# Moments by ScalarE for the first four token tiles, and a norm without GpSimd's long step for the last four, in the ConvFFN of a two-layer encoder

## The chip, the cores and the metric

One core of one Trainium2 chip. The metric is device microseconds of one execution of the program, as a median over runs; the profile is one more execution with the hardware profiler on.

## The reference

The model is a two-layer post-norm encoder over 1024 tokens of width 1024, in float32. Each layer is an attention mixer and then a ConvFFN, each with a residual and a LayerNorm behind it. The change touches the LayerNorm behind the ConvFFN, once in each layer:

```python
def _layer_norm(x, g, b):
    mu = jnp.mean(xf, axis=-1, keepdims=True)
    var = jnp.mean(jnp.square(xf - mu), axis=-1, keepdims=True)
    y = (xf - mu) * lax.rsqrt(var + LN_EPS)
    return y * g + b
...
x = _layer_norm(DN_ALPHA * x + h, ln_attn_g[layer], ln_attn_b[layer])
f = _conv_ffn(x, ffn_w_in[layer], ffn_conv_w[layer], ffn_conv_b[layer], ffn_w_out[layer])
x = _layer_norm(DN_ALPHA * x + f, ln_ffn_g[layer], ln_ffn_b[layer])
```

## The kernel before

The 1024 tokens are eight tiles of 128 rows, `Y[0]` to `Y[7]`, each 128x1024. The down projection of the ConvFFN is made as seven products of a Strassen-like scheme. Each product runs over 11 steps of the contraction, and a step makes 12 matmuls: four token tiles, three matmuls each (high by high, high by low, low by high). The matmuls of a product gather in four PSUM banks, `As` (name `dna`) or `Cs` (name `dnc`). In this text the steps of the last product are called p4(0) to p4(10), after the function that prepares them; the product ahead of it is the one into the second `Cs`.

A step is prepared so: `pair` loads two 128x512 blocks into one tile `pr` by two DMAs from SP's queue (L646); for p4 VectorE then subtracts an earlier block from the second (L713); ScalarE rounds the tile to its high part (L654); VectorE subtracts for the low part (L655). The two parts lie in a tile `opj`, of which there are seven, so preparation runs up to seven steps ahead of TensorE.

The tile `pr` comes from `room`, which goes round a ring of eight buffers with three tags:

```python
def room():
    tag = ("raw", "raw", "whi", "wlo", "whi", "wlo", "whi", "wlo")[ring["pr"] % 8]
    ring["pr"] += 1
    return wpool.tile([P, 2, 512], F32, name="pr", tag=tag, bufs=2 if tag == "raw" else 3)
```

When the last product begins, `room` has been called 64 times, so p4(0) has a buffer of tag raw. The same three tags serve other code: in layer 0 the weights `b_v_weights(0)` for the next layer, which the program asks for behind p4(3), take two buffers of each tag, and hold theirs in whi and wlo until a product long after.

The order of the instructions on each engine and queue is made ahead of time by a planner that plays the program through with planned durations and, whenever an engine is free, places the ready instruction that stands first in the program. A tile has no buffer until its first writer is placed, and the buffers of one tag are given out in the order in which the program asks for them: a tile's first writer is not placed ahead of the first writer of a tile of the same tag asked for earlier. Once placed, an engine keeps its order. `urgent()` moves an instruction some 400 places forward in that order.

At the end of the last `Cs` product `to_y` (L677) adds the four banks to `Y[0]` to `Y[3]`, and `layer_norm` is called for them: two `bn_stats` of 512 columns (L211), `bn_aggr` (L213), two 128x1 steps on GpSimd (L215, L216), two `scalar_tensor_tensor` of 1024 columns on VectorE (L229, L231), and a store (L235). In the program these stand ahead of p4(0). The last product then runs steps 0 to 4 over all four token tiles, and steps 5 to 10 tile by tile. As each bank is finished, `to_y` (L675) and `layer_norm` follow for `Y[4]` to `Y[7]`. For t < 3 in layer 1 (`Y[4]`, `Y[5]`, `Y[6]`) `spread` is true: ScalarE scales and shifts (L225), VectorE multiplies by the gain (L226), GpSimd adds the bias row over 1024 columns (L227). For the others VectorE does L229 and two halves of L231, each stored by itself (L233). In layer 0 `tail` also turns each finished tile by eight transposes (L245, name `tps`) for the next layer.

Of the kernel before, what the change touches and what calls it, by code (L numbers as in the profile page):

```python
# [10 lines left out]
F32 = mybir.dt.float32  # L11
F32R = mybir.dt.float32r
AF = mybir.ActivationFunctionType
ALU = mybir.AluOpType
# [6 lines left out]
P = 128  # L21
S = 1024
D = 1024
# [7 lines left out]
EPS = 1e-5  # L31
# [63 lines left out]
def trunk_kernel(ctx, tc, A):  # L95
    nc = tc.nc
# [18 lines left out]
    sm = ctx.enter_context(tc.tile_pool(name="sm", bufs=6))  # L115
# [29 lines left out]
    mhalf = const.tile([P, 1], F32, name="mhalf")  # L145
# [59 lines left out]
    def moments(y, halves=None):  # L205

        st = sm.tile([P, 2, 6], F32, name="st", tag="st", bufs=3)
        for h in (1, 0) if halves else (0, 1):
            if halves:
                halves(h)  # L210
            nc.vector.bn_stats(st[:, h, :], y[:, h * 512:(h + 1) * 512])  # L211
        mv = sm.tile([P, 2], F32, name="mv", tag="mv", bufs=3)
        nc.vector.bn_aggr(mv, st.rearrange("p a b -> p (a b)"))  # L213
        rs = sm.tile([P, 1], F32, name="rs", tag="rs", bufs=3)
        nc.gpsimd.tensor_scalar(rs, mv[:, 1:2], 1.0, EPS, ALU.mult, ALU.add)  # L215
        nc.gpsimd.tensor_tensor(rs, rs, mhalf, ALU.pow)  # L216
        return mv[:, 0:1], rs

    def layer_norm(y, g_bc, b_bc, out=None, spread=False, halves=None):

        mean, rs = moments(y, halves)
        if spread:
            nm = sm.tile([P, 1], F32, name="nm", tag="nm", bufs=3)
            nc.gpsimd.tensor_scalar(nm, mean, rs, -1.0, ALU.mult, ALU.mult)
            nc.scalar.activation(y, y, AF.Identity, bias=nm, scale=rs)  # L225
            nc.vector.tensor_tensor(y, y, g_bc, ALU.mult)  # L226
            nc.gpsimd.tensor_tensor(y, y, b_bc, ALU.add)  # L227
        else:
            nc.vector.scalar_tensor_tensor(y, y, mean, g_bc, ALU.subtract, ALU.mult)  # L229
            for c in (slice(0, 512), slice(512, D)) if halves else (slice(0, D),):  # L230
                nc.vector.scalar_tensor_tensor(y[:, c], y[:, c], rs, b_bc[:, c], ALU.mult, ALU.add)  # L231
                if halves and out is not None:
                    nc.sync.dma_start(out=out[:, c], in_=y[:, c])  # L233
        if out is not None and (spread or not halves):
            nc.sync.dma_start(out=out, in_=y)  # L235
# [92 lines left out]
    def ffn(layer, op, old, four, xp, tmp, then, out, tail):  # L328
# [222 lines left out]
        room = old.tile([P, 8192], F32R, name="late", tag="xs1")  # L551
# [70 lines left out]
        Y = [fp.tile([P, D], F32, name=f"y{t}") for t in range(NT)]  # L622
        g_bc = fp.tile([P, D], F32, name="g_bc")
        b_bc = fp.tile([P, D], F32, name="b_bc")
# [13 lines left out]
# [4 lines that stand above are left out]
# [20 lines left out]
        def times(ps, o, t, first, last):  # L662
            a, b = [[x[:, 0], x[:, 1]] for x in o] if isinstance(o, list) else [
                [o[:, n, c:c + 512] for c in (0, 512)] for n in range(2)]
            a = [x[:, t * P:(t + 1) * P] for x in a]
            mm3(ps, [(a[0], a[1], b[0], b[1])], first=first, last=last, joined=True)
# [5 lines left out]
        def to_y(t, c, ps, first):  # L672
            with urgent():
                if first:
                    nc.vector.scalar_tensor_tensor(Y[t][:, c], Y[t][:, c], ALPHA, ps, ALU.mult, ALU.add)  # L675
                else:
                    nc.vector.tensor_tensor(Y[t][:, c], Y[t][:, c], ps, ALU.add)  # L677
# [70 lines left out]
            new_x(xp2)  # L748
        for t in range(4):
            to_y(t, lo_, Cs[t], False)  # L750
            layer_norm(Y[t], g_bc, b_bc, out(t))
        for m in range(NM - 6):
            turn(As, p4(m), m)
            if m:
# [2 lines left out]
        for t in range(4):  # L757
            for m, o in enumerate(os):
                times(As[t], o, t, False, m == 5)

            def add(h, t=t):
                if not h:
                    to_y(t + 4, lo_, As[t], True)

            layer_norm(Y[t + 4], g_bc, b_bc, out(t + 4), t < 3 and layer == 1, add)
            tail(t + 4, Y[t + 4], fp)

    def score_tile(W, T, i, q, ka, kb, mask, out, fold):
# [590 lines left out]
    def tail_a(t, y, f):  # L1359
# [6 lines left out]
        if t == 7:  # L1366
            plain(b_v(0, wv0, lambda: 0.0, f, range(0, 4)))
            for p in pend:
                x_from(*p, "SS")

    ffn(0, op, xp, (top, ("hl1", "hl0", "g", "b")), xp2, tmp, then_a, lambda t: x2_d[t], tail_a)
    open_f.pop().close()
    st_xb = open_f.pop()
# [16 lines left out]
    def then_b():  # L1390
# [8 lines left out]
        return x, f  # L1399

    ffn(1, op, xp, (keep, ("rt", "hl", "cosT", "sinT")), xp2, tmp, then_b, lambda t: A["out"][t * P:(t + 1) * P, :],
        lambda t, y, f: None)
    open_f.pop().close()
# [69 lines left out]
```

## Time and profile before

| | |
|---|---|
| median of 3 runs | 2545.67 us (2541.77 to 2546.02) |
| the profiled execution's own time | 2547.09 us |
| its span, first to last instruction | 2545.3 us |
| mean granted TensorE clock | 0.985 |
| busy: TensorE, VectorE, ScalarE, GpSimd | 96%, 74%, 46%, 23% |

A row of a timeline gives the start in us from the span's start, the duration, engine, line, operation and operands, and in brackets the idle time of that engine just before and what ended it. "x4" means that so many like instructions are merged in the row. PE is TensorE, PEld its weight load, DVE VectorE, ACT ScalarE, POOL GpSimd, SP the queue that issues the DMAs.

### The profile page before, as it was taken

The numbers are of one execution on the slowest core, as the hardware profiler recorded it, in microseconds if no ns is written. First come the engines' busy times: TensorE is split into PE (matmuls) and PEld (weight loads), VectorE is DVE, ScalarE is ACT, GpSimd is POOL, SyncE is SP. The second block draws the span as 40 slices with busy tenths as digits, with TensorE's granted clock in tenths as the row PEclk, the third lists the DMA queues.
The fourth block names the chain that finished last, engine by engine and source line by source line (L and its number), as shares of the span: only waits on it lengthen the run. The fifth ranks groups of instructions, "written<-read, shape, count | busy, mean of one in ns | idle before, by whom it ended". The sixth has DMA issues, their size and how long they took to land.

```text
span 2545.3 us, 36019 instructions
## 1 busy us (share of the span) xinstructions
PE 2452.3 (96%) x12784; PEld 2094.7 (82%) x12784; DVE 1888.5 (74%) x3446; ACT 1164.3 (46%) x2077; POOL 588.6 (23%) x670
## 2 busy tenths in 40 slices
PE   8999999899999999999999999998999999999997
PEld 7989898777778888788788898987777888887885
DVE  5656565768887877787858686878688888787877
ACT  3545454533544544443325454544334554544432
POOL 3333332621200000000123536355312000100003
PEclk9999999999999999999999999999999999999998
DMA  7564655634522222755465546454545222228552
GB/s 243 182 215 132 201 157 179 207 113 168 196 105 99 83 79 99 262 181 195 139 205 170 161 144 193 144 181 135 175 158 185 89 96 91 83 87 302 170 194 100
DMA packets 195172, 400.76 MB, mean 157 GB/s; under 512 B 18976, under 2 KB 73248, under 8 KB 193968
## 3 DMA queue, kind: packets, MB, share of 16 engines
q1 hardware_dynamic: 194992, 398.46, 46.8%
q8 instruction: 101, 1.65, 0.3%
q14 instruction: 79, 0.65, 0.1%
HBM read 285.07 MB, written 113.31 MB: 157 GB/s over the span
## 4 chain that ended last, share of the span: by engine, by line
PE 79%; DMA 9%; DVE 6%; POOL 2%; issue 2%; ACT 1%; SPq 1%; POOLq 0%; DVEq 0%; ACTq 0%
PE ua L192 15%; PE pj L192 10%; PE dna L192 8%; PE uc L192 8%; PE vp L192 7%; PE dnc L192 7%; PE op L192 6%; PE ub L192 4%; PE tp L813 3%; DMA t<-in_w_dram 3%; PE sc L783 2%; PE sc L784 2%; PE pv L1211 2%; DMA t1d<-t 1%; PE pv L1007 1%
## 5 line engine op out<-in xcount | busy, mean ns | idle before, releaser
L192 PE MATMUL pj<-x,whi 128*128 128x512 f32 x992 | 322.2, 397 | 0.2 <-DVE rt L1149 0.2
L192 PE MATMUL dna<-opj 128*128 128x512 f32 x1008 | 235.7, 395 | 10.2 <-DVE opj L659 5.7
L192 PEld LDWEIGHTS dna<-opj 128*128 128x128 f32 x1008 | 191.7, 191 | 52.5 <-DVE opj L659 6.6
L192 PEld LDWEIGHTS pj<-x,whi 128*128 128x128 f32 x992 | 184.3, 189 | 34.9 <-issue 0.2
L818 DVE TENSOR_TENSOR tl<-tp,th 128x512 fp32r<-128x512 f32 (+1 forms) x240 | 149.9, 633 | 72.0 <-ACT th L817 67.0
L529 POOL TENSOR_TENSOR he<-he,tg 128x512 f32<-128x512 f32 x22 | 49.2, 2234 | 659.0 <-DVE tg L527 629.0
L192 PE MATMUL vp<-whi,x 128*128 128x256 f32 (+1 forms) x960 | 194.7, 289 | 3.1 <-DVE vt L1107 2.0
L192 PE MATMUL pj<-x,wlo 128*128 128x512 f32 x496 | 197.4, 398 | 0.0
L817 ACT CAST th<-tp 128x512 fp32r<-128x512 f32 (+1 forms) x240 | 127.8, 542 | 129.8 <-PE tp L813 87.3
L192 PE MATMUL dnc<-opj 128*128 128x512 f32 x792 | 180.5, 389 | 0.0
L192 PEld LDWEIGHTS dnc<-opj 128*128 128x128 f32 x792 | 148.7, 188 | 30.8
L192 PE MATMUL op<-wo,oh 128*128 128x512 f32 x512 | 165.7, 404 | 8.3 <-DVE yw L302 3.2
L654 ACT CAST opj<-pr 128x1024 fp32r<-128x1024 f32 x88 | 92.7, 1054 | 152.6 <-PE dna L192 64.2
L813 PE MATMUL tp<-ident_r,pt 128*128 128x128 f32 x864 | 152.8, 278 | 8.7 <-DVE tl L818 6.5
L446 ACT CAST late<-sr 128x512 fp32r<-128x512 f32 x132 | 81.2, 618 | 172.4 <-DVE sr L452 142.0
L192 PEld LDWEIGHTS vp<-whi,x 128*128 128x128 f32 x960 | 154.1, 190 | 6.7 <-DVE vt L1107 2.2
L1001 POOL TENSOR_SCALAR pt<-pt,rr 128x128 f32<-128x128 f32 (+7 forms) x128 | 96.2, 758 | 220.7 <-DVE rr L1000 190.7
L215 POOL TENSOR_SCALAR rs<-mv 128x1 f32<-128x1 f32 x32 | 18.4, 575 | 541.8 <-DVE mv L213 540.9
L783 PE MATMUL sc<-ka,q 128*128 128x512 f32 (+3 forms) x384 | 133.4, 372 | 8.9 <-DVE pt L1185 5.0
L1189 ACT ACTIVATE pt<-pt,mn 128x256 f32<-128x256 f32 (+7 forms) x128 | 98.9, 773 | 86.6 <-DVE mn L794 63.5
L998 ACT ACTIVATE pt<-pt,mn 128x128 f32<-128x128 f32 (+7 forms) x128 | 99.1, 775 | 85.5 <-DVE mn L794 67.1
L192 PE MATMUL vp<-wlo,x 128*128 128x256 f32 (+1 forms) x480 | 138.2, 288 | 0.0
(255 smaller groups left out, 6560.5 us busy)
## 6 DMA issues: line engine op xcount, KB each, us to landing
raw<-in_w_dram SPq DMA_DIRECT2D x88, 512.0 KB, 4.4
pr<-in_w_dram SPq DMA_DIRECT2D x132, 256.0 KB, 3.4
pr<-hd SPq DMA_DIRECT2D x96, 256.0 KB, 3.0
t<-in_w_dram SPq DMA_DIRECT2D x22, 512.0 KB, 3.6
hd<-tg SPq DMA_DIRECT2D x22, 512.0 KB, 3.0
raw<-in_aqk_dram SPq DMA_DIRECT2D x16, 512.0 KB, 4.9
vd<-vt SPq DMA_DIRECT2D x32, 256.0 KB, 2.8
qd<-hl SPq DMA_DIRECT2D x32, 256.0 KB, 3.5
```

The source lines that it names most:

```text
L192: nc.tensor.matmul(ps, a, b, start=first and i == 0, stop=last and i == n - 1, skip_group_check=joined)
L446: nc.scalar.copy(w[:, 0], src)
L654: nc.scalar.copy(o[:, :, 0:512], rs[0])
L783: nc.tensor.matmul(ps[:, :n], q, ka[:, c0:c0 + n], start=True, stop=False)
L784: nc.tensor.matmul(ps[:, :n], q, kb[:, c0:c0 + n], start=False, stop=not dg)
L813: nc.tensor.transpose(tp[:, n * P:(n + 1) * P], pts[q][:, k * P:(k + 1) * P], ident)
L817: nc.scalar.copy(th[:, :n], tp[:, :n])
L818: nc.vector.tensor_tensor(tl[:, :n], tp[:, :n], f32(th[:, :n]), ALU.subtract)
L998: nc.scalar.activation(pt, pt, AF.Exp, bias=mn, scale=-1.0, accum_out=rs)
L1001: nc.gpsimd.tensor_scalar(pt, pt, rr, 1.0, ALU.mult, ALU.mult)
L1189: nc.scalar.activation(pt, pt, AF.Exp, bias=mn, scale=-1.0, accum_out=rs)
L1211: nc.tensor.matmul(o, vv[:, k, v, :], t[:, c], start=(k == 0 and m == 0), stop=(g == j and b == 1 and m == 2))
```

## The change

The first four tiles of each ConvFFN get a norm of their own: ScalarE runs over the tile twice with an accumulated sum (once for the mean, once squared for the variance), GpSimd makes three 128x1 steps, and VectorE's two passes remain. The output of the squaring pass is not needed; it goes to a tile from `room`. For the last four tiles `spread` is now false in both layers.

```diff
+    def layer_norm_act(y, g_bc, b_bc, out, junk):
+        s = sm.tile([P, 4], F32, name="as", tag="as", bufs=3)
+        nc.scalar.activation(y, y, AF.Identity, accum_out=s[:, 0:1])
+        nc.gpsimd.tensor_scalar(s[:, 1:2], s[:, 0:1], -1.0 / D, 0.0, ALU.mult, ALU.add)
+        nc.scalar.activation(junk, y, AF.Square, bias=s[:, 1:2], accum_out=s[:, 2:3])
+        nc.gpsimd.tensor_scalar(s[:, 3:4], s[:, 2:3], 1.0 / D, EPS, ALU.mult, ALU.add)
+        nc.gpsimd.tensor_tensor(s[:, 3:4], s[:, 3:4], mhalf, ALU.pow)
+        nc.vector.scalar_tensor_tensor(y, y, s[:, 1:2], g_bc, ALU.add, ALU.mult)
+        nc.vector.scalar_tensor_tensor(y, y, s[:, 3:4], b_bc, ALU.mult, ALU.add)
+        nc.sync.dma_start(out=out, in_=y)
...
         for t in range(4):
             to_y(t, lo_, Cs[t], False)
-            layer_norm(Y[t], g_bc, b_bc, out(t))
+            layer_norm_act(Y[t], g_bc, b_bc, out(t), room().rearrange("p a n -> p (a n)"))
...
-            layer_norm(Y[t + 4], g_bc, b_bc, out(t + 4), t < 3 and layer == 1, add)
+            layer_norm(Y[t + 4], g_bc, b_bc, out(t + 4), False, add)
```

## Rows read from the trace of the kernel before

**Rows 1.** The page: busy time of each engine, share, instructions.

```profile
PE 2452.3 (96%) x12784; PEld 2094.7 (82%) x12784; DVE 1888.5 (74%) x3446; ACT 1164.3 (46%) x2077; POOL 588.6 (23%) x670
```

**Rows 2.** Chain that ended last, layer 1's end: start us, us, what.

```profile
2466.63 29.92 PE dnc L192 x132
2496.55 29.93 PE dna L192 x132
...
2532.54 1.04 POOL rs L215
...
2537.41 2.82 DVE y L231
```

**Rows 3.** Windows by stage: us, busy us (count) by engine, clock, DMA.

```profile
1239.85:1276.00 36.15, 33.57 (x159) 27.38 (x158) 35.98 (x49) 10.17 (x13) 7.35 (x8) 1.00 0.43 147
...
2496.50:2526.50 30.00, 29.97 (x133) 24.48 (x131) 28.72 (x41) 5.48 (x6) 7.78 (x13) 1.00 0.18 71
2526.50:2545.30 18.80, 0.00 (x0) 0.00 (x0) 11.61 (x9) 3.41 (x3) 12.72 (x10) 0.60 0.28 112
```

**Rows 4.** Timeline of VectorE in layer 1's last stage.

```profile
2521.52 1.28 DVE L675 SCALAR_TENSOR_TENSOR y<-y,dna 128x512 f32<-128x512 f32 x2 [0.82 <-PE dna L192]
...
2530.17 3.36 DVE L229 SCALAR_TENSOR_TENSOR y<-y,mv,g_bc 128x1024 f32<-128x1024 f32 x1
...
2537.41 3.48 DVE L231 SCALAR_TENSOR_TENSOR y<-y,rs,b_bc 128x512 f32<-128x512 f32 x2 [2.74 <-POOL rs L216]
```

**Rows 5.** Timeline of TensorE in layer 0's last product.

```profile
1259.99 1.09 PE L245 MATMUL tps<-ident_r,y 128*128 128x128 f32 x8 [0.94 <-DVE y L231]
1261.67 1.19 PE L192 MATMUL dna<-opj 128*128 128x512 f32 x4 [0.59 <-ACT opj L654]
...
1264.79 5.06 PE L192 MATMUL dna<-opj 128*128 128x512 f32 x21 [1.06 <-DVE opj L655]
```

**Rows 6.** Timeline of SP's queue: layer 1's last load of p4.

```profile
2490.70 0.43 SPq L646 DMA_DIRECT2D pr<-in_w_dram  x1
```

**Rows 7.** Groups by line and form, VectorE, 2490 to 2546: busy us, mean ns.

```profile
L655 DVE TENSOR_TENSOR opj<-pr,opj 128x1024 fp32r<-128x1024 f32 x9 | 10.9, 1208 | 0.0
L211 DVE BATCH_NORM_STATS2 st<-y 128x6 f32<-128x512 f32 x15 | 9.9, 673 | 0.0
...
L231 DVE SCALAR_TENSOR_TENSOR y<-y,rs,b_bc 128x1024 f32<-128x1024 f32 x4 | 5.0, 1269 | 0.0
...
L213 DVE BATCH_NORM_AGGREGATE mv<-st 128x2 f32<-128x12 f32 x8 | 1.6, 194 | 0.0
L713 DVE TENSOR_TENSOR pr<-pr,t 128x512 f32<-128x512 f32 x2 | 1.4, 692 | 1.8 <-DMA pr<-in_w_dram 1.6
```

**Rows 8.** Groups by line, ScalarE, whole span (of L654, 2490 to 2546).

```profile
L998 ACT ACTIVATION_READ_ACCUMULATOR pt<-pt,mn 128x1 f32 x128 | 24.1, 188 | 0.0
L225 ACT ACTIVATE y<-y,nm,rs 128x1024 f32<-128x1024 f32 x5 | 6.1, 1239 | 24.3 <-POOL nm L224 24.3
L515 ACT ACT_TABLE_LOAD x2 | 2.6, 1283 | 6.2 <-DVE tg L512 6.2
...
L654 ACT CAST opj<-pr 128x1024 fp32r<-128x1024 f32 x7 | 7.4, 1055 | 11.7 <-PE dna L192 6.7 <-PE dnc L192 3.3 <-DVE pr L713 1.7
```

**Rows 9.** The page, DMA issues: KB each, median us to landing.

```profile
pr<-in_w_dram SPq DMA_DIRECT2D x132, 256.0 KB, 3.4
```

**Rows 10.** Timeline of GpSimd: its 128x1 step, alone and beside VectorE.

```profile
2502.96 0.19 POOL L215 TENSOR_SCALAR rs<-mv 128x1 f32<-128x1 f32 x1 [182.12 <-DVE mv L213]
...
2507.21 1.11 POOL L215 TENSOR_SCALAR rs<-mv 128x1 f32<-128x1 f32 x1 [0.98 <-DVE mv L213]
```

**Rows 11.** Windows where layer 1's down projection begins.

```profile
2316.00:2320.00 4.00, 1.19 (x4) 0.67 (x4) 3.86 (x5) 3.92 (x8) 0.75 (x1) 1.00 1.05 395
2320.00:2324.00 4.00, 2.55 (x7) 2.03 (x8) 4.00 (x6) 1.53 (x4) 0.84 (x1) 0.77 1.06 389
2324.00:2328.00 4.00, 4.00 (x16) 3.17 (x15) 4.00 (x8) 3.52 (x8) 0.00 (x0) 0.81 1.04 417
```

## The prediction

> **What bounds the kernel now.** I read the page first: TensorE is busy for 96% of the span and no other engine for more than 74% [rows 1]. So an edit on VectorE, ScalarE or GpSimd counts only where TensorE waits for them, and behind its last matmul. I then looked for those places in the two stretches that the diff touches.
>
> In layer 1 there is no wait ahead of the end. The last two products take 29.92 and 29.93 us for 132 matmuls each, which is 0.227 us a matmul with no gap [rows 2]. Then TensorE is done, at 2526.5, and the span goes on for 18.8 us [rows 2, 3]. That tail is VectorE and GpSimd: two banks are only taken up at 2521.5; one L229 takes 3.36 us beside GpSimd's long step, where a pass of 1024 columns alone takes 1.27; and the last L231 waits 2.74 us for a 128x1 step which stood in GpSimd's queue behind such long steps, then takes 3.48 us for its two halves [rows 2, 4, 7].
>
> In layer 0 VectorE is busy for 35.98 of the 36.15 us of the last product, and TensorE stands idle three times, 0.94, 0.59 and 1.06 us, together 2.6 [rows 3, 5].
>
> A third thing is to be seen in SP's queue: the last of p4's loads is issued at 2490.7, 6 us before the product ahead of p4 ends at 2496.55 [rows 2, 6]. The eleven steps of the last product are all fetched early; that is why it starts without a gap.
>
> **The change, part by part.** *VectorE, first four tiles.* Eight L211 and four L213 a layer go: 8 x 0.67 + 4 x 0.19 = 6.1 us [rows 7]. In layer 1 that is off the path, since TensorE did not wait; in layer 0 it can at most give back the 2.6 us.
>
> *ScalarE, first four tiles.* Each gets two passes. The nearest row is L225's pass of 1024 columns, 1.24 us, and an accumulated sum adds an instruction of 0.19 [rows 8]: 1.43 us a pass, eight passes, 11.4 us a layer. ScalarE has the time on average; the question is what is queued behind them. Square may also need a table load, of which the trace does not show whether it is due behind Silu: between 0 and 1.28 us a layer [rows 8]. I take 0, because Identity of L225 ran behind Silu without one, and keep both ends. The Trainium skill (ScalarE: Activation LUTs, section "What ACT_TABLE_LOAD costs") puts a switch of sets at about 2.66 us, the drain included. By that page the sum would be up to 5.3 us more; the row shows only the 1.28 of the load itself.
>
> *The buffer for the squares.* This is the part that decides. `room` is called four times more, ahead of p4(0). By the ring, the four squaring outputs take raw, raw, whi, wlo, and p4(0) to p4(10) now get whi, wlo, whi, wlo, raw, raw, whi, wlo, whi, wlo, whi. Buffers of a tag are given out in program order, and a tile's first writer is not placed ahead of that of an earlier tile of its tag. So the load of p4(0) is placed behind the third tile's Square, that of p4(1) behind the fourth's, and p4(4) and p4(5) behind the first two. These loads were out 6 us before the end of the product ahead; now they are placed after it.
>
> How late: call E the end of the product ahead. Its first bank is finished nine matmuls before E (9 x 0.227 = 2.0 us), and `to_y` takes 0.64 [rows 2, 4], so ScalarE starts at E - 1.4. A Square needs the mean of its own tile through GpSimd, 0.19 to 1.11 us for the step [rows 10], so the planner puts another tile's pass in between: Identity 0, 1, Square 0, 1, Identity 2, 3, Square 2, 3. The third Square starts after six passes, at E - 1.4 + 8.6 = E + 7.2. Then p4(0) needs two issues (0.43 each at most) and 3.4 us to land [rows 6, 9], L713 0.69, L654 1.06: TensorE's first matmul at E + 13.2. From below: SP need not wait for the third Square itself, only for what stands ahead in its queue, the loads of p4(4) and p4(5), which need the first two Squares done (E + 4.3); then ScalarE's own queue sets it, eight passes to E + 10.0 and the rounding, 11 us. From above: with the roundings of p4(4) and p4(5) ahead (2.1 us) 15.3, and the low part of p4(0) comes 1.2 us after [rows 7, 8]. I take a gap of 12.5 us in each layer, range 11 to 16.
>
> *The clock.* Where layer 1's down projection starts, TensorE worked for 1.19 of 4 us at full clock, and in the next 8 us its granted clock was 0.77 and 0.81, that is, it stood at the lower level, 1.2 GHz, for a part of them: 4 x 0.23 + 4 x 0.19 = 1.7 us lost [rows 11]. The new gap is longer; I charge 1.7 us a layer.
>
> *Layer 0's sum.* 12.5 + 1.7 = 14.2, less the three idle times of before (2.6), less the transposes of about two finished tiles, which the planner can put into the gap (2 x 1.05 = 2.1, from [rows 5]): + 9.5 us. Behind it TensorE goes on with the next layer, busy for 96% of the span [rows 1], so the loss stays.
>
> *Layer 1's sum.* TensorE ends at 2496.55 + 12.5 + 29.93 + 1.7 = 2540.7. By then all the steps lie ready, so the matmuls run tile by tile as the program has them, and `Y[4]` to `Y[6]` are normed while TensorE works. Without GpSimd's long steps only `Y[7]` is left: L675 0.64, L211 0.67, L213 0.19, L229 1.27, L231 in halves 1.3, together 4.1 us [rows 4, 7]; GpSimd's two steps hide behind L229. From the last VectorE instruction to the end it was 2545.3 - 2540.9 = 4.4 us [rows 3, 4]; I keep that. The end is 2549.2, + 3.9: the tail shrinks from 18.8 to 8.5, which gives back 10.3 of 14.2. The three more stores cost nothing, as they go out under the matmuls; without that cover each is 0.43 us of SP.
>
> *Total.* + 13.4 us. The profiled execution's own time is 2547.09, so 2560.5 for one like it; it lies 1.4 above the median of 2545.67, and so I say 2559 for the median.
>
> **The rivals.** *The loads are not held.* If later tiles of a tag may take a free buffer while an earlier one has no writer yet, only p4(4) and p4(5) wait, for the first two Squares, and come in just by the time TensorE reaches them. Then there is no gap: layer 0 gives back up to 2.6 us, and in layer 1 VectorE goes from 2521.5 through four tiles of 4.1 - about 16 us, 2538, then 4.4 - to 2542, a gain of 3.3. Up to 5.9 us faster, 2540 to 2544. For it speaks that buffers are free by then; against it the planner's rule. It decides from a gap of nothing. Chance 0.13, half of it past the bound of 0.2% (5.1 us), which is about what a measurement of this kernel can tell from no change.
>
> *The gap is there but nearly paid for.* With a gap of 8 to 9 us, shorter than my lower bound (if the planner squares the third tile sooner), no loss by the clock and four tiles' transposes in layer 0's gap, layer 0 costs some 2 and layer 1 gives some 1 back: 2545 to 2550. Chance 0.08.
>
> *A second wait in layer 0.* The weights for the next layer take the raw buffers behind the squares, and p4(4) and p4(5) stand behind the weights; their rounding and subtraction go onto ScalarE and VectorE (1.06 and 1.21 us for each), VectorE being full there. If that holds p4(4), or the weights' roundings go ahead of p4(0)'s, another 4 to 10 us come on top: 2563 to 2570. Chance 0.17.
>
> The forecast, 2551 to 2563, has 0.62.
>
> **How the numbers follow.** Slower by over 0.2% are the forecast, the second wait and a small part of the paid-for gap: 0.80. Within: the rest of the paid-for gap and half of the free loads: 0.13. Faster: 0.07. The range goes from 2546 (beyond it the free loads and part of the paid-for gap) to 2570 (16 us of gap in both layers and a second wait, or both table loads on top).
>
> **What would show it.** Right: in both layers TensorE idle for 11 to 16 us between the last `dnc` matmul and the first `dna` matmul, ended by ScalarE's rounding or VectorE's low part; p4's first loads in SP's queue some 4 to 8 us after E; no GpSimd step of over 2 us in the tail, which is 8 to 9 us long; L229 and L231 there at 1.27. Wrong, if the loads of p4(0) to p4(3) are out before E and the last product of layer 1 takes 30 us as before; then the tail alone decides, and the time falls.

## The result: 1.7% slower, outside the forecast range

After the change the median is 2589.05 us (2588.0 to 2591.25, four runs) against 2545.29 (2541.77 to 2546.02) before on the same chip: ratio 1.0166, 95% interval 1.0151 to 1.0182, that is 38 to 46 us. The forecast was + 13.4 and at most 2570. The direction was right, the size was not, and, as the runs show, a whole cause was missing.

The page after: TensorE is still the busiest by far, as in [rows 1], busy for 29 us more at the same 96%.

```profile
PE 2481.4 (96%) x12784; PEld 2098.2 (81%) x12784; DVE 1876.8 (73%) x3428; ACT 1178.8 (46%) x2106; POOL 594.6 (23%) x672
```

The windows after by stage, which answer to [rows 3]: layer 0's last product, layer 1's last product, and the tail behind the last matmul.

```profile
1238.00:1291.10 53.10, 42.22 (x182) 34.40 (x182) 41.87 (x50) 26.00 (x36) 9.11 (x13) 0.84 0.53 178
2522.10:2576.10 54.00, 36.41 (x133) 27.86 (x132) 41.22 (x49) 18.76 (x25) 15.23 (x17) 0.75 0.42 146
2576.10:2586.20 10.10, 0.04 (x1) 0.00 (x0) 6.13 (x9) 0.00 (x0) 3.04 (x4) 0.64 0.28 105
```

Layer 0's last product went from 36.15 to 53.10 us (its last matmuls end 0.4 us behind this window), layer 1's from 30.00 to 54.00, the tail from 18.80 to 10.10, and the clock in the two products from 1.00 to 0.84 and 0.75. TensorE's timeline in layer 1, the part that answers to the chain of [rows 2]:

```profile
2492.05 30.08 PE L192 MATMUL dnc<-opj 128*128 128x512 f32 x132
2531.68 2.07 PE L192 MATMUL dna<-opj 128*128 128x512 f32 x4 [9.55 <-ACT opj L666]
2536.57 3.78 PE L192 MATMUL dna<-opj 128*128 128x512 f32 x8 [2.81 <-DVE opj L667]
2542.92 2.08 PE L192 MATMUL dna<-opj 128*128 128x512 f32 x4 [2.57 <-ACT opj L666]
2547.65 28.50 PE L192 MATMUL dna<-opj 128*128 128x512 f32 x116 [2.65 <-DVE opj L667]
```

There is not one gap but four, 17.6 us together, and four matmuls between them take 2.07 us where at full clock they would take about 1.1. The same engine in layer 0, answering to [rows 5]:

```profile
1244.90 1.97 PE L257 MATMUL tps<-ident_r,y 128*128 128x128 f32 x8 [6.87 <-DVE y L228]
1247.08 2.07 PE L192 MATMUL dna<-opj 128*128 128x512 f32 x4 [0.20 <-ACT opj L666]
...
1256.03 1.19 PE L192 MATMUL dna<-opj 128*128 128x512 f32 x4 [1.02 <-ACT opj L666]
1259.18 1.94 PE L257 MATMUL tps<-ident_r,y 128*128 128x128 f32 x8 [1.96 <-DVE y L228]
```

The product ahead ends at 1238.03, so p4(0)'s first matmul comes 9.05 us after it. The first tile's transposes (`tps`) lie inside that wait and do not make it: the matmul starts right behind its own rounding, which ends at 1247.02.

```profile
1245.99 1.03 ACT L666 CAST opj<-pr 128x1024 fp32r<-128x1024 f32 x1
```

The same holds for the 1.96 us at 1259.18: the matmuls behind those transposes start at 1260.82, when a low part (L667, 1259.55 to 1260.76) is done.

What holds the steps, by the chain that ended last (start us, us, what):

```profile
2520.13 0.70 DVE y L689
...
2520.85 3.23 ACT y L222 x6
2524.08 1.14 ACT pr L224 x2
...
2525.29 1.30 POOL as L225
2526.66 1.47 POOL as L226
...
2531.38 2.69 POOL as L226
...
2535.30 0.21 DVE opj L667
...
2535.53 3.32 DMA pr<-hd
...
2540.08 3.31 DMA pr<-hd
```

ScalarE's passes come first, then GpSimd's 128x1 steps one behind the other, then loads. What releases the loads is not always the row above them. The load at 2535.53 starts when ScalarE's fourth Square is done (at 2535.51; the low part L667 that started at 2535.30 ends only at 2536.5), and this Square had itself waited 2.63 us for GpSimd:

```profile
2534.26 1.15 ACT L224 ACTIVATE pr<-y,as 128x1024 f32<-128x1024 f32 x1 [2.63 <-POOL as L223]
```

The load at 2540.08 does wait for a low part (L667) of VectorE. SP's queue, answering to [rows 6] (the end of the product ahead is 2522.1):

```profile
2497.90 0.33 SPq L658 DMA_DIRECT2D pr<-hd  x1
...
2502.74 0.33 SPq L658 DMA_DIRECT2D pr<-hd  x1
...
2525.24 0.33 SPq L658 DMA_DIRECT2D pr<-hd  x1
...
2529.48 0.34 SPq L229 DMA_DIRECT2D out_dram<-y  x1
2529.87 0.43 SPq L658 DMA_DIRECT2D pr<-hd  x1
```

By the order of SP's instructions these are the loads of p4(0) and p4(2), both long before; p4(4), 3.1 us after; and p4(1), which stands behind p4(4) to p4(6) and behind the store of the first normed tile. The loads of p4(4), p4(5) and p4(6) each wait for one of the first three Squares.

That accounts for the two last products. The span grew by 40.9 us (2545.3 to 2586.2), and these two, with the tail, make 30 of it, worked out below. The rest is in stretches where the diff changes no instruction. One product of twelve matmuls in the up projections, `uc<-late,whi`, in the timelines of before (first line layer 0, second layer 1):

```profile
765.72 2.88 PE L192 MATMUL uc<-late,whi 128*128 128x512 f32 x12
...
2081.66 2.88 PE L192 MATMUL uc<-late,whi 128*128 128x512 f32 x12
```

and after:

```profile
778.42 2.88 PE L192 MATMUL uc<-late,whi 128*128 128x512 f32 x12
...
2082.43 2.96 PE L192 MATMUL uc<-late,whi 128*128 128x512 f32 x12
```

In layer 1 it takes 2.96 us instead of 2.88, at full clock and without a gap. Over the whole up projection, the mean time from one matmul's start to the next (of all such times between 215 and 300 ns) went from 226.8 to 231.5 ns in layer 0 and from 226.8 to 231.8 in layer 1; in the attention mixer of layer 1 from 230.1 to 234.2. Below this is called the pace.

### The profile page after: what moved, and what is told of

Same layout as the page of the kernel before. It is cut to its first block, busy times and chain, and to the rows that moved or that the text cites. A ratio compares the mean times of both kernels' runs of the same rounds, so it can differ in the third digit from the quotient of the medians.

```text
span 2586.2 us, 36013 instructions
## 1 busy us (share of the span) xinstructions
PE 2481.4 (96%) x12784; PEld 2098.2 (81%) x12784; DVE 1876.8 (73%) x3428; ACT 1178.8 (46%) x2106; POOL 594.6 (23%) x672
## 4 chain that ended last, share of the span: by engine, by line
PE 80%; DMA 9%; DVE 5%; POOL 2%; issue 2%; ACT 1%; SPq 0%; POOLq 0%; DVEq 0%; ACTq 0%
PE ua L192 15%; PE pj L192 11%; PE dna L192 8%; PE uc L192 8%; PE dnc L192 7%; PE vp L192 7%; PE op L192 6%; PE ub L192 4%; PE tp L825 3%; DMA t<-in_w_dram 3%; PE sc L795 3%; PE sc L796 2%; PE pv L1223 2%; DMA t1d<-t 2%; PE pv L1019 1%
## 5 line engine op out<-in xcount | busy, mean ns | idle before, releaser
L192 PE MATMUL dna<-opj 128*128 128x512 f32 x1008 | 244.5, 404 | 27.3 <-ACT opj L666 13.3
L666 ACT CAST opj<-pr 128x1024 fp32r<-128x1024 f32 x88 | 92.0, 1050 | 137.5 <-PE dna L192 63.9
L667 DVE TENSOR_TENSOR opj<-pr,opj 128x1024 fp32r<-128x1024 f32 x88 | 107.1, 1221 | 48.2 <-ACT opj L666 48.2
L524 DVE SCALAR_TENSOR_TENSOR tv<-uv,cw,tv 128x1023 f32<-128x1023 f32 x88 | 115.9, 1317 | 32.7 <-ACT tv L522 32.3
```

The source lines that it names most:

```text
L192: nc.tensor.matmul(ps, a, b, start=first and i == 0, stop=last and i == n - 1, skip_group_check=joined)
L524: nc.vector.scalar_tensor_tensor(t[:, j:], u[:, :S - j], cw[:, 2 - j, k:k + 1], t[:, j:], ALU.mult, ALU.add)
L666: nc.scalar.copy(o[:, :, 0:512], rs[0])
L667: nc.vector.tensor_tensor(o[:, :, 512:1024], rs[0], f32(o[:, :, 0:512]), ALU.subtract)
```

## Experiments

Theory: two causes that add up. (1) The squares' buffers from the ring hold back the steps of the last product. (2) The new tag `as`, three tiles of 128x4, takes 96 bytes of each partition (three times 32, of which 16 are used) in a pool that lies ahead of most tiles of the left side of SBUF; those tiles move, and matmuls that read a moved tile together with one that did not move are slower. Rivals: ScalarE's eight passes make the gaps by themselves; the slower pace came from something else. Medians of before differ from chip to chip (2544.6 to 2551.6 us), so ratios to before on the same chip are given, with 95% intervals; they lie up to 0.2% off the quotient of the two medians printed beside them.

**shift_alone.** On the kernel before:

```diff
+        for t in range(3):
+            nc.gpsimd.memset(sm.tile([P, 4], F32, name="as", tag="as", bufs=3), 0.0)
```

> The kernel before with one thing of the change alone: the three 128x4 tiles of the new tag, 96 bytes of each partition in the pool of small tiles, are set to zero once and never read, so every tile that is allocated behind them on the left side of SBUF lies 96 bytes further; the instructions of TensorE, VectorE, ScalarE and SyncE are those of before, in the same order. Theory (the places of the operands set the pace of some products): the matmuls of the two up projections take 231.6 ns instead of 226.7, as after the change, the up projection of layer 1 takes 10 us more, and the total is 2552 to 2556. Rival (the slower pace came from something else of the change, or from that execution): 2544 to 2547, and 226.7 ns.

Measured: 2563.59 us against 2549.47, ratio 1.0043 (1.0025 to 1.0061); pace 231.6 and 231.9 ns in the two up projections, 234.2 in the attention mixer of layer 1. The total came out above the 2552 to 2556 that I expected. The product shown above is as slow as after the change:

```profile
2093.63 2.96 PE L192 MATMUL uc<-late,whi 128*128 128x512 f32 x12
```

The last product of layer 1 has no idle time, as before. The shift is a cause by itself and costs about 11 us (6 to 16).

**places_kept.** On the change:

```diff
-        s = sm.tile([P, 4], F32, name="as", tag="as", bufs=3)
+        s = sm.tile([P, 4], F32, name="as", tag="st", bufs=3)
```

> The change with its sums in the existing tag of 128x2x6 tiles, so that every other tile lies where it lay before; the squares still go to the buffers of the ring. Theory (two causes that add up): the up projections run at 226.7 ns, the last products keep their gaps (some 17 us longer than before in layer 0 and 24 in layer 1), and the total is 2577 to 2582. Rival (places do nothing): 2587 to 2591. Rival (places did most of it): under 2565.

Measured: 2574.89, ratio 1.0091 (1.0073 to 1.0108); pace 226.8 and 226.9. Idle in the two last products 12.2 and 19.4 us. A little less than I expected: the change without its shift costs 23 us (19 to 28). With the shift's 11 (6 to 16) that is 34 (25 to 44) against the change's 38 to 46: with these intervals the two causes are enough.

**own_tile.** On the change, a 128x1024 tile in the down projection's pool:

```diff
+            junk = fp.tile([P, D], F32, name="junk")
...
-            layer_norm_act(Y[t], g_bc, b_bc, out(t), room().rearrange("p a n -> p (a n)"))
+            layer_norm_act(Y[t], g_bc, b_bc, out(t), junk)
```

> The change with the squares written to a 128x1024 tile of their own in the pool of the down projection, so that the ring of the loads is as before; the 96 bytes of the new tag stay. Theory (the ring held back the loads): the last product of layer 1 starts within 1 us of the end of the product ahead and takes 30 to 31 us, that of layer 0 36 to 38; what is left is the shift, and the total is 2548 to 2554. Rival (ScalarE's eight passes ahead of the roundings make the gaps by themselves): gaps of 8 us or more stay in both layers, 2570 to 2589.

Measured: 2549.26, ratio 1.0002 (0.9982 to 1.0023). There is no idle time in either last product; they take 33.6 us in layer 0 and 29.9 in layer 1, where the 132 matmuls follow each other:

```profile
2496.64 30.08 PE L192 MATMUL dna<-opj 128*128 128x512 f32 x132
```

ScalarE still makes the same eight passes in each layer: its queue now has them between the roundings of the later steps, no longer ahead of them all. So the passes alone do no harm.

**own_tile_places_kept.** Both edits.

> Both edits of the two runs before: squares to a tile of their own, and the sums in the existing tag. Theory (held loads and shifted places are all there is): no gap, 226.7 ns in the up projections, a tail shorter by some 3 to 10 us; 2538 to 2545. Rival (the moments on ScalarE delay its roundings at the start of the last product): 2548 to 2565.

Measured: 2542.79, ratio 0.9973 (0.9954 to 0.9993); no idle time, pace 226.9, last product of layer 0 33.5 us, tail 11.7. Without its two side effects the change is a gain. The four kernels make a table of two by two: the ring costs 1.6% with the shift (1.0166 against 1.0002) and 1.2% without (1.0091 against 0.9973), the shift 0.7% with the ring and 0.3% without, 0.43% on before. The intervals overlap, so two causes that add fit; that they add exactly is not shown.

**four_sums.** On the change, a tile of sums for each of the four token tiles, places kept:

```diff
+            sums = [fp.tile([P, 4], F32, name=f"as{t}") for t in range(4)]
...
-            layer_norm_act(Y[t], g_bc, b_bc, out(t), room().rearrange("p a n -> p (a n)"))
+            layer_norm_act(Y[t], g_bc, b_bc, out(t), room().rearrange("p a n -> p (a n)"), sums[t])
```

> The change with a 128x4 tile of sums for each of the first four token tiles, in the pool of the down projection, instead of three buffers in turn; all other tiles lie where they lay before, and the squares still go to the ring. Theory A (the fourth tile's moments wait for the first tile's to be finished, because there are only three buffers, and with them the loads behind the fourth square): TensorE's idle time in the last product of layer 1 falls from 19.4 us in places_kept to 10 to 14, and the total from 2575 to 2560 to 2570. Theory B (the eight passes of ScalarE ahead of the first rounding, and GpSimd's steps, are what counts): within 3 us of places_kept, 2572 to 2578.

Measured: 2574.12, ratio 1.0115 (1.01 to 1.013). Idle time in layer 1's last product 13.5 us, as theory A said; total as theory B said. That the fourth tile waits for a buffer of sums can be seen after the change:

```profile
2529.54 1.06 ACT L222 ACTIVATE y<-y 128x1024 f32<-128x1024 f32 x1 [2.07 <-DVE y L228]
...
2530.60 1.03 ACT L666 CAST opj<-pr 128x1024 fp32r<-128x1024 f32 x1
```

but that wait is not what costs the time. Why 6 us less idle (and a last product of 46.6 us instead of 55.4) do not show in the total stays open; the profiled execution's up projection of layer 1 was 9.6 us longer than that of places_kept, at the same pace (TensorE stood idle there for 8.8 us instead of 5.4, and the clock granted was 0.98 instead of 1.00), and the tail 1.7. No instruction of that stretch was edited.

**squares_01_in_ring** and **squares_23_in_ring.** On own_tile_places_kept, the ring stepped on by four, with two of the four squares in its buffers (for the second `t > 1`):

```diff
+            if t > 1:
+                ring["pr"] += 1
+            r = room().rearrange("p a n -> p (a n)") if t < 2 else junk
...
```

> As ring_moved (all tiles in the places of before, the ring stepped on by four), but the squares of the first two token tiles are written to the ring's two raw buffers; those of the other two go to the tile of their own. Theory (the harm comes from the steps that TensorE takes first: with whi and wlo free, the planner rounds p4(0) to p4(3) ahead of the moments and only p4(4) and p4(5) are late): gaps in the last product of each layer under 8 us, total 2540 to 2556. Rival (two held buffers of four do half the harm): 2556 to 2566.

> The other half: the squares of the third and fourth token tile in the ring's whi and wlo, those of the first two in the tile of their own. Theory (the steps p4(0) to p4(3) go through whi and wlo, and ScalarE's eight passes stand ahead of their roundings): the gaps of the change come back nearly whole, total 2562 to 2578. Rival (half the harm): 2552 to 2561.

Measured: 2565.72, ratio 1.0066 (1.0045 to 1.0088), and 2564.97, ratio 1.0074 (1.0048 to 1.0100). Idle in the last products 6.1 and 8.0 us in the first, 11.2 and 14.7 in the second. By the totals my distinction failed, and the first met the rival's forecast: against own_tile_places_kept (0.9973) all four squares in the ring cost 1.2% (places_kept), either pair 0.9 to 1.0%. By the two last products the pairs do differ. Against own_tile_places_kept these lost 10.2 and 11.5 us with the first pair, 15.7 and 20.6 with the second, 16.3 and 25.5 with all four (in layer 0 up to the next layer's first product `pj`, in layer 1 up to TensorE's end). The totals come out alike because the up projection of layer 1, which neither edit touches, took 433.2 us in the first and 419.2 in the second, with 14.0 and 4.8 us idle; why stays open, as in four_sums. With the first pair the waits come in the middle of the product, after 48 of its 132 matmuls, at p4(4) and p4(5), which wait for the raw buffers:

```profile
2511.35 11.04 PE L192 MATMUL dna<-opj 128*128 128x512 f32 x48
2525.60 1.20 PE L192 MATMUL dna<-opj 128*128 128x512 f32 x4 [3.21 <-ACT opj L670]
2531.59 21.34 PE L192 MATMUL dna<-opj 128*128 128x512 f32 x80 [4.79 <-DVE opj L671]
```

**ring_moved.** On own_tile_places_kept, `ring["pr"] += 1` ahead of each call: the same tags as in the change, nothing written to them.

> Squares to a tile of their own, all tiles in the places of before, but the ring is stepped on by four without anything being written, so the loads of the last product go to the same tags as in the change (whi, wlo, whi, wlo, raw, raw, ...). Theory (a buffer that is held does the harm, not the order of the tags): as own_tile_places_kept, 2538 to 2546, no gap. Rival (the last product needs its first loads in the raw buffers, which come free first): gaps in the last product, 2555 or more.

Measured: 2537.27, ratio 0.9972 (0.9959 to 0.9984), 0.7 us below what I expected, and no idle time:

```profile
2496.17 30.08 PE L192 MATMUL dna<-opj 128*128 128x512 f32 x132
```

It is the held buffer, not the order of the tags.

**last_four** (on before, `False` in place of `t < 3 and layer == 1`) and **first_four** (own_tile_places_kept with that condition put back) take the two parts of the change apart.

> The kernel before with the second part of the change alone: the last four token tiles of layer 1 normed by VectorE, none of it on GpSimd but the 128x1 steps. Theory (the tail was set by GpSimd's long steps): the tail behind the last matmul falls from 18.8 us to 12 to 16, total 3 to 6 us below before. Rival (VectorE has too much to do there with the first four tiles' statistics still its own): the tail stays at 17 to 20 us, total within 2 us of before.

> The first part of the change alone, with squares to a tile of their own and the sums in the existing tag: moments of the first four token tiles by ScalarE, the last four normed as before. Theory (VectorE is eased in layer 0, where it was full; in layer 1 GpSimd's long steps still set the end): layer 0 gives back 2 to 3 us, the tail stays at 15 to 19 us, total 1 to 5 us below before. Rival (no gain without both parts): within 1 us of before.

Measured: 2538.29, ratio 0.9970 (0.9957 to 0.9984), and 2535.48, ratio 0.9968 (0.9956 to 0.9980). The tail is 14.9 us in both, 11.7 with both parts; layer 0's last product is 36.1 and 33.6. Each part gains about 8 us, within 4 of what its stages show (3.9; 3.9 + 2.4), and more than I expected (3 to 6 and 1 to 5). In first_four GpSimd's long steps are still there and the tail fell to 14.9 all the same, where I had 15 to 19: a part of the tail of before was work of VectorE that had piled up. Both together do not gain measurably more than either alone.

**pad32, pad64, pad128, pad256.** shift_alone with one, two, four and eight tiles.

> shift_alone with 32 bytes instead of 96 (one 128x4 tile), read by the median time from one matmul's start to the next in the two up projections. If any shift of some tiles against the others slows the products: 231 to 234 ns for the products that read a shifted tile. If it goes by steps of 64 bytes (96 and 32 leave the same rest): 231 to 234 too. If places did nothing: 226.7.

> shift_alone with 64 bytes instead of 96. If it goes by steps of 64 bytes: 226.7 ns in both up projections, as before. If any shift does it, or steps of 128 bytes: 231 to 234 ns.

> shift_alone with 128 bytes. Shifts of 32 and 96 bytes gave 231.2 to 231.9 ns as the mean of an up projection, 64 bytes 229.1 to 230.4. If it goes by steps of 128 bytes: 226.7 ns in both, as before. If any shift of some tiles against the others slows the products: 229 to 234 ns.

> shift_alone with 256 bytes (eight 128x4 tiles). Shifts of 32, 64, 96 and 128 bytes all slowed the up projections (229.1 to 231.9 ns), and a shift of both operands together left the pace of their product at 227. If the distance between the two operands counts by steps of 256 bytes: 226.7 to 227 ns in both up projections and a total within 4 us of before. If any shift of one against the other does it: 229 to 234 ns, and 8 to 17 us more.

**all_left_96.** On before, a shift of the whole left side:

```diff
-    nc.gpsimd.memset(shift.tile([P, 8], F32, name="shift0"), 0.0)
+    nc.gpsimd.memset(shift.tile([P, 32], F32, name="shift0"), 0.0)
```

> The kernel before with 96 bytes added to the first small tile on the left side, so that all tiles of the left side, the weights' pool among them, lie 96 bytes further, and those of the right side where they were; the instructions are those of before in the same order. Theory (the difference between the places of a product's two operands counts): in layer 0 the products of b1h with whi and wlo (both moved) go back to 226.9 ns, those of late with whi and of t with wlo (one moved) rise to 233; in layer 1 b1h with whi and wlo (one moved) rise to 233, late with whi and t with wlo (both moved) go back to 226.7. Rival (the place itself counts, a moved tile is slow): whi and wlo are in all of these, so all are 230 to 235 in both layers. Rival (it is the accesses of other engines, not the operands): no such pattern by operands.

Measured, mean pace in ns in the up projections of layer 0 and layer 1, and the time of one run (of pad256 the median). Before on the same chips took 2550.17 us for pad32 and pad64 (median), 2551.61 for pad128 and all_left_96 (one run) and 2546.32 for pad256 (median):

```
kernel        layer 0   layer 1   us
before        226.8     226.8
pad32         231.2     231.4     2560.15
pad64         229.1     230.4     2558.14
shift_alone   231.6     231.9     2563.59 (median)
pad128        230.9     230.9     2562.29
pad256        226.8     226.9     2545.76 (ratio 1.0005, 0.9993 to 1.0017)
all_left_96   231.8     231.4     2566.32
```

A shift of 256 bytes is free, the four smaller ones cost 2 to 5 ns a matmul; pad64 fell between its two forecasts. By product (mean ns, layer 0 / layer 1; shift_alone moves b1h and t12h in layer 0, t and late in layer 1, and not the weights' whi and wlo; all_left_96 moves whi and wlo too):

```
product     before         shift_alone    all_left_96
b1h, wlo    227.0 / 226.9  234.0 / 229.3  227.2 / 233.7
b1h, whi    226.9 / 227.7  234.1 / 228.9  231.0 / 235.0
late, whi   226.7 / 226.7  227.4 / 233.6  234.2 / 227.0
t, wlo      226.9 / 226.9  229.4 / 233.3  233.8 / 228.9
t12h, late  227.0 / 227.1  234.2 / 233.9  233.4 / 234.1
t, late     226.8 / 226.8  229.7 / 230.4  230.1 / 228.8
```

Where one operand moved, 233 to 235; where both or neither did, 227 to 231. The timeline of all_left_96 shows the table turned over, layer 0 slow and layer 1 fast:

```profile
766.01 2.97 PE L192 MATMUL uc<-late,whi 128*128 128x512 f32 x12
...
2096.29 2.88 PE L192 MATMUL uc<-late,whi 128*128 128x512 f32 x12
```

and that of pad256 is as before:

```profile
776.98 2.88 PE L192 MATMUL uc<-late,whi 128*128 128x512 f32 x12
...
2096.70 2.88 PE L192 MATMUL uc<-late,whi 128*128 128x512 f32 x12
```

So it is the distance between the two operands that counts, and not the place. Open is why products with both or neither moved still lose 2 to 4 ns: t with late, and b1h with whi, which I expected back at 226.9 in layer 0 of all_left_96, where both moved. No other distance past 128 bytes than 256 was tried.

## Why the prediction was wrong

**Right.** TensorE sets the time, and the squares' buffers do the harm: with them elsewhere no gap is left (own_tile, ring_moved). ScalarE starts its passes 1.25 us ahead of the end of the product (2520.85 against 2522.1; I had 1.4), and the first matmul's wait ends with its rounding (L666). A pass costs a quarter less than I took (1.43), 1.04 to 1.13 us from one to the next, since most of the 0.187 for a sum lies under the next pass:

```profile
L224 ACT ACTIVATE pr<-y,as 128x1024 f32<-128x1024 f32 x8 | 9.1, 1137 | 2.7 <-POOL as L223 2.6
L222 ACT ACTIVATE y<-y 128x1024 f32<-128x1024 f32 x8 | 8.4, 1050 | 37.0 <-DVE y L689 33.3 <-DVE y L228 3.6
```

The third Square came after five passes, not six. No table load was added (six before and six after), as I took it, so no run here bears on the 2.66 us that the Trainium skill (ScalarE: Activation LUTs, section "What ACT_TABLE_LOAD costs") gives for a switch of sets. In the tail no step of GpSimd is over 2 us, and the lines that took 3.36 and 3.48 [rows 4] take:

```profile
2579.72 1.28 DVE L241 SCALAR_TENSOR_TENSOR y<-y,mv,g_bc 128x1024 f32<-128x1024 f32 x1
2581.73 1.41 DVE L243 SCALAR_TENSOR_TENSOR y<-y,rs,b_bc 128x512 f32<-128x512 f32 x2 [0.72 <-POOL rs L216]
```

**Wrong: "Then p4(0) needs two issues (0.43 each at most) and 3.4 us to land".** The sum of the gap goes through a late load of p4(0), and its load was not late. It was issued 24 us ahead of the end of the product, p4(2)'s 19 us ahead, and VectorE stood idle for 14.70 us with the blocks in place. What held p4(0) was its place in the queues of VectorE and ScalarE. Its subtraction (L725) stands behind the first tile's whole norm (L227, L228):

```profile
2520.13 2.73 DVE L689 TENSOR_TENSOR y<-y,dnc 128x512 f32<-128x512 f32 x4 [14.70 <-PE dnc L192]
...
2528.17 1.28 DVE L228 SCALAR_TENSOR_TENSOR y<-y,as,b_bc 128x1024 f32<-128x1024 f32 x1 [0.44 <-POOL as L226]
2529.37 0.68 DVE L725 TENSOR_TENSOR pr<-pr,t 128x512 f32<-128x512 f32 x1
```

Its rounding, at 2530.60, stands behind seven of ScalarE's eight passes, the seventh of which waited 2.07 us for that norm (the rows in four_sums). This is near the bound from below that I gave, ScalarE's own queue, and not the load that I summed up. "So the load of p4(0) is placed behind the third tile's Square" is neither shown nor refuted by it: the order fits the planner's rule, as what follows p4(0) is placed behind the third Square, and SP, having nothing to wait for there, would still issue the load early. It fits, too, that in squares_01_in_ring, where no Square takes whi or wlo, nine of the eleven steps are subtracted ahead of the end of the product at 2511.4, the ninth at 2507.81 and the tenth at 2521.53:

```profile
2507.81 0.69 DVE L729 TENSOR_TENSOR pr<-pr,t 128x512 f32<-128x512 f32 x1 [0.96 <-DMA pr<-in_w_dram]
...
2521.53 0.68 DVE L729 TENSOR_TENSOR pr<-pr,t 128x512 f32<-128x512 f32 x1
```

But when the planner placed what is not in the runs, so this reason is argued and not shown. The loads of p4(1) and p4(3) came behind those of p4(4) to p4(6) and the first store.

**Mis-sized: "I take a gap of 12.5 us in each layer".** The first gap was shorter, 9.55 us in layer 1. But I let the rest run without a gap ("by then all the steps lie ready"), and it had three more, 8.0 us: the steps right behind the first had waits of their own. **Mis-sized: "I charge 1.7 us a layer" for the clock.** Layer 1's last product took 54.0 us, of which 17.6 are idle and 29.9 the matmuls at full clock [rows 2]; 6.5 are left for the clock, granted at 0.75 over the stage. The clock stood at its lower level (1.2 GHz) from 2524.4 to 2551.7, half of the stage, in which the four gaps lie with a few matmuls between them. Layer 1's sum: 17.6 + 6.5 = 24.1 lost (I had 14.2); the tail 10.1 (I had 8.5), so 8.7 given back: + 15.4, not + 3.9. In the tail VectorE needs 7.0 us behind TensorE's end, where I had 4.1: it is still at the tile ahead, and GpSimd's two steps, which I had hidden behind L229 (now L241), outlast it, so the last tile's L243 waits 0.72 us for them. The end comes 3.1 us behind VectorE's last instruction, where I had 4.4.

**Mis-sized: layer 0's "+ 9.5 us".** The next layer's first product, `pj`, started 65.84 us after the start of the last product before (1305.69 - 1239.85) and 80.54 after (1318.54 - 1238.0): + 14.7. Of this, 8.8 is idle time (13.4 instead of 4.6) and 5.9 the clock, granted at 1.00 throughout before and at its lower level here from 1241.0 to 1251.2 and from 1258.0 to 1264.9. My idle terms made 7.8 (12.5 less 2.1 and 2.6), so it was again the 1.7 us for the clock that was short. Transposes did fill a part of the gap, as I let them. The rival "a second wait in layer 0" had the sign and the size (4 to 10 on top) by luck: the idle time is only 1.0 above my sum, and the rest is clock.

Together 15.4 + 14.7 = 30.1 instead of 13.4. Of the 16.7 that are missing, 9.0 are the clock in both layers, 6.1 idle time and 1.6 the tail. **Missing: the 96 bytes.** The other 10.8 of the span's 40.9 us agree with what shift_alone measured, 11 (6 to 16), closer than that interval can tell. I had the line with the new tag before me and counted it as three small tiles; a price for where it stands in the pool was in no row of before, and I had no rival for it. The source of before had a sign of it: three tiles, `shift0` to `shift2`, which are set to zero and never read, so that all they can do is to move the tiles behind them.

## What to carry to other kernels

A scratch output that takes a buffer from a ring of load buffers can hold back whoever comes next in that ring: give it a tile of its own, or count what is late behind it to the last step, not to the first, and on every engine that the step needs, not on its load alone. A new small tile in a pool moves everything behind it: look at the pace of matmuls in stages that the edit does not touch, and keep the distance between the operands of a product at what it was; a change of it by 256 bytes is the one tried here that cost nothing. Where two edits are made together, run each alone: here each gains 0.3%, and what came with them made a loss of 1.7% of it.

## What the runs showed of the hardware

The pace of 128x512 matmuls at full clock depends on how far apart the tiles of the two operands lie: the pace in the up projections was 226.8 ns in before and 226.8 to 226.9 after a shift by 256 bytes, 229.1 to 231.9 after 32, 64, 96 or 128, and 233 to 235 in the single products where one operand moved by 96. The Trainium skill (TensorE: Matmul & The Clock Gate, section "Step-by-step: what each phase is for") says that loading the next weights takes no read bandwidth from the running matmul, and (SBUF — State Buffer, section "Who interferes with whom") that TensorE waits for nobody; by that the shift would cost nothing, and the measurement decides: shift_alone cost 0.43%.

GpSimd's 128x1 step on `rs` took 0.19 us alone [rows 10] and in the tail 1.28 beside L241:

```profile
2579.77 1.28 POOL L215 TENSOR_SCALAR rs<-mv 128x1 f32<-128x1 f32 x1 [2.38 <-DVE mv L213]
```

It ends 0.05 us behind L241, which started 0.05 us earlier. The Trainium skill (SBUF — State Buffer, section "Who interferes with whom") says that a VectorE instruction with two inputs in SBUF contends with a GpSimd instruction that reads SBUF; the trace agrees. In layer 1's last product a chain of such steps, one of them 2.69 us long, held ScalarE's fourth Square for 2.63 us, and the load at 2535.53 waited for that Square.
